# A hybrid encoder layer on one core: a written-out instruction order in place of a planner's, and four attention chunks held open

## The chip, the cores and the metric

The kernel runs on one core of a Trainium2 chip. The core has TensorE for matrix products (PE; its weight loads are listed as PEld), VectorE (DVE), ScalarE (ACT), GpSimd (POOL) and SyncE (SP), which issues most DMAs. Engines run their own instruction lists in order and wait for each other through semaphores. The metric is the device time of one execution in microseconds; before the change the median of three runs is 1474.67 us (1472.99 to 1477.0).

## The reference

One layer, 2048 tokens of width 1024, batch 1, all in f32:

```python
hn = rmsnorm(h, mix_norm_g)
u, g_ssm, q, k, v, g_attn = split(hn @ w_in)            # six parts of 512 columns
y_ssm = s5_branch(u, ...) * silu(g_ssm)                 # diagonal complex state space, 32 groups of 16 channels, then GELU and GLU
y_att = stick_breaking_branch(q, k, v, ...) * silu(g_attn)
h = h + concat([y_ssm, y_att]) @ w_out
h = h + sigmoid(rmsnorm(h) @ w_ple_gate) * (p @ w_ple_proj)
```

The attention has 8 heads of 64 and no softmax. For each query the weight of an earlier key is `sigmoid(z)` times the product of `sigmoid(-z)` over the keys between the two, strictly causal, in blocks of 128 queries. The S5 branch is a linear recurrence over time with complex state, computed in chunks.

## The kernel before, in words

Precision comes from splitting: an f32 matrix becomes a high and a low half in f32r, and `mm3` or `mm3x` adds three products of halves (lines 541 to 543 and 707 to 709). Where no split is made, plain f32 products run: the S5 products `ps_b` (L401) and `ps_y` (L461 to L464), the transposes `ps_pack` (L340, L352) and `ps_t` (L1000), and `ps_o` of the attention (L843).

The program is written stage by stage, in this order:

- `phase_u`: the tokens are loaded, normalised, transposed (`ps_x`) and split into `xt`; the 512 columns of `u` are computed (`ps_u`), 256 tokens at a time, and POOL stores them (`u<-uq`, L638). For the first 256 tokens the input comes already transposed (`load_plain`); their norms are found by `norms` through PE (`ps_row`, L579 and L585) and applied later. Beside it DVE computes the S5 constants in `ssm_chain`, some 250 short instructions.
- Eight S5 batches, each beside one `gate_unit`, which computes the S5 gates (`ps_sg`).
- The attention, 40 steps over four pairs of heads, the pairs 8 steps apart. `attn_proj` computes q, k, v and the gate of 128 tokens (`ps_q`, transposes `ps_tq`), each product cut in two halves of 64 rows that run side by side. `attn_block` handles 128 queries of a pair of heads. For each chunk of 512 keys, from the latest back, PE makes scores `ps_z`; ACT takes the sigmoid into `px` (L816); DVE forms the running products in place (L821); PE transposes `px` into `ps_wt` (L526, 64 x 64 pieces); ACT copies that to a `ws` tile (L835). The products with v, `ps_o` (L843), add up over all chunks in one PSUM bank. The code puts them out for `HOLD` chunks at a time, 128 rows by 64 columns each, which is the other way of halving the array.
- In the last ten attention steps the GLU of the S5 branch (`ps_g2`, `ps_v2`; the page shows these as `ps_g` and `ps_v`) and sums of weight blocks are worked in.
- `phase_out`: `mixed_pair` multiplies by `w_out` (`ps_h`), `gated_pair` transposes (`ps_t`) and multiplies by `w_ple_gate` (`ps_g`) and `w_ple_proj` (`ps_p`), seven products in place of eight, as in Strassen's scheme. `yr` are the split operands.

The order in which an engine runs its instructions is not that of the program. `arrange` takes the whole list, `plan` finds each instruction's dependences and gives it a length by a table in `duration`, `best_order` runs a list scheduler forwards and backwards six times and keeps the best of its own estimates, and `arrange` then fixes the order of every engine by a chain of dependences. Groups marked by `abreast` stay together. The rings that bound how far work runs ahead are sizes in one line: `PXB` (8 `px` tiles), `WSB` (5 `ws` tiles of 4 KB a partition).

[...]

Of the kernel before, what the change touches and what calls it, by code (L numbers as in the profile page):

```python
# [18 lines left out]
P = 128  # L19
# [4 lines left out]
G = 32  # L24
GH = 16
ST = 64
L = 16
# [13 lines left out]
XB, XTB, GTB, QSB, PXB, WSB, SWB, ROTB, STA, STB, STC, ALT, ALT0, ALT1, SSM_STEPS, SSM_DEPTH, PREP0, PXX, WSX, XTX, XT0 = 4, 2, 5, 5, 8, 5, 2, 2, 3, 2, 3, "o", 0, 30, 10, 2, 0, 0, 0, 0, 13  # L41
# [8 lines left out]
HOLD = 2  # L50
# [1231 lines left out]
def footprint(ap, offset, shape):  # L1282

    row = 1
    for n in shape[1:]:
        row *= n
    p0, m = offset // row, 1
    f = offset % row + sum((n - 1) * s for s, n in ap[1:] if s < 0)
    for s, n in ap[1:]:
        if s and n > 1:  # L1290
            m = sum(m << (abs(s) * k) for k in range(n)) if n * abs(s) > 64 or m != 1 or s not in (1, -1) else (1 << n) - 1
    return p0, p0 + ap[0][1], m << f


def duration(i, name, outs, ins, psum):

    n = max([a[1] for a in outs + ins] or [1])
    eng = str(i.engine).split(".")[-1]
    if name == "InstDMACopy":
        names = [a.bass_ap.tensor.name for a in i.ins if getattr(a, "bass_ap", None) is not None]  # L1300
        return (0.6 if eng == "Pool" else 0.45), (4.0 if any("ssm_w_glu" in k for k in names) else 0.0)
    if name == "InstMatmult":
        cols, kind = outs[0][1], ins[0][2]
        if i.is_transpose:
            return (0.031 if ins[0][0] <= 64 else 0.109), 0.11
        if "float32r" in kind or "bfloat16" in kind:
            return max(cols / 2400.0 + 0.0136, 0.107) / (2 if ins[0][0] <= 64 else 1), 0.11
        half = min(outs[0][0], ins[0][0]) <= 64
        return (0.5 if outs[0][0] <= 32 else 1 if half else 2) * max(cols / 1160.0, 0.056), 0.12
    if eng == "Activation":  # L1310
        return (0.05 if psum else 0.094) + n * 0.00083, 0.065 if psum else 0.03
    if eng == "Pool":
        if name == "InstTensorTensor" and "pow" in str(i.op).lower():
            return 0.35 + 0.15 * n, 0.08
        base, slope = {"InstMemset": (0.04, 0.0008), "InstTensorCopy": (0.4, 0.001), "InstTensorScalarPtr": (0.25, 0.001), "InstTensorScalarAffineSelect": (0.14, 0.0008)}.get(name, (0.12, 0.00186))
        return base + slope * n, 0.09
    if name == "InstTensorScalarPtr" and i.is_tensor_tensor_scan:
        return 0.05 + n * 0.0022, 0.03
    if name in ("InstMemset", "InstTensorCopy", "InstTensorScalarPtr") and not psum and not i_tt(i):
        return 0.07 + n * 0.0006, 0.03  # L1320
    return 0.07 + n * 0.00104, 0.03


def i_tt(i):

    return getattr(i, "is_scalar_tensor_tensor", False)


def plan(tc, pools):

    mybir_i = list(tc.nc.cur_bb.bb.instructions)
    first, last = 16512, 229344
    open_l, open_r, open_b, base, slots, spans, over, home, used = [], [], [], {}, {}, [], {}, {}, {}
    for p in sorted(pools, key=lambda p: p.id):
        kb = int(p.kb_per_partition_size() * 1024)
        sp = str(p.space).split(".")[-1]
        if sp == "DRAM":
            base[p.id] = 0
        else:
            side = open_b if sp == "PSUM" else open_r if "right" in str(p.side) else open_l  # L1340
            born = int(p.alloc_inst.name.split("-")[1])
            while side and side[-1][2] is not None and side[-1][2] < born:
                side.pop()
            at = side[-1][0] if side else 0 if side is open_b else last if side is open_r else first
            lo = at - kb if side is open_r else at
            end = p.release_inst
            side.append((lo if side is open_r else lo + kb, p.id, None if end is None else int(end.name.split("-")[1])))
            base[p.id] = lo
            for q, l2, h2, e2, s2 in spans:
                if sp == s2 and l2 < lo + kb and lo < h2 and e2 is not None and int(e2.name.split("-")[1]) < int(p.alloc_inst.name.split("-")[1]):  # L1350
                    over.setdefault(p.alloc_inst.name, []).append(e2.name)
            spans.append((p.id, lo, lo + kb, end, sp))
        for sp, size, tag, addr, _ in p.gen_slots(0):
            home[tag] = p.alloc_inst.name, p.release_inst.name if p.release_inst is not None else None
            slots.setdefault(tag, []).append((str(sp).split(".")[-1], base[p.id] + addr, size // P))
    turn, tiles, held, pre, length, opened, soft, mode = {}, {}, {}, [], [], {}, [], {}
    number = {i.name: k for k, i in enumerate(mybir_i)}
    for k, i in enumerate(mybir_i):
        if type(i).__name__ == "BassTilePoolBoundary":
            pre.append(set())  # L1360
            soft.append({number[q] for q in over.get(i.name, [])} | used.get(i.name, set()))
            length.append((0.0, 0.0, 0, False))
            continue
        need, ins, outs, loose, psum, read = set(), [], [], set(), False, 0
        for w, accs in ((0, i.ins), (1, i.outs)):
            for a in accs:
                b = getattr(a, "bass_ap", None)
                if b is None:
                    continue
                t, n = b.tensor, 1  # L1370
                ap = [(int(s), int(c)) for s, c in b.ap]
                for s, c in a.ap[1:]:
                    n *= int(c)
                (outs if w else ins).append((int(a.ap[0][1]), n, str(a.dtype)))
                read += not w and n > 1 and type(t).__name__ == "Tile" and slots_space(slots, t.tag) == "SB"
                if type(t).__name__ != "Tile":
                    continue
                shape = tuple(int(x) for x in t.shape)
                if t.name not in tiles:
                    mine = slots[t.tag]  # L1380
                    q = turn[t.tag] = turn.get(t.tag, -1) + 1
                    sp, lo, size = mine[-q % len(mine)]
                    tiles[t.name] = rec = (sp, [], [], k)
                    if t.tag in opened:
                        loose.add(opened[t.tag])
                    opened[t.tag] = k
                    if sp != "DRAM":
                        kept = []
                        for l2, h2, r2 in held.get(sp, []):
                            if l2 < lo + size and lo < h2:  # L1390
                                need.update(r2[2])
                                if lo <= l2 and h2 <= lo + size:
                                    continue
                            kept.append((l2, h2, r2))
                        held[sp] = kept + [(lo, lo + size, rec)]
                sp, accesses, users, born = tiles[t.name]
                loose.add(born)
                a0, r0 = home[t.tag]
                loose.add(number[a0])
                used.setdefault(r0, set()).add(k)  # L1400
                if sp == "PSUM":
                    psum = True
                    f = (0, P, 1)
                    w = 1
                elif sp == "DRAM":
                    row = shape[-1] if len(shape) < 3 else shape[1] * shape[2]
                    o = int(b.offset)
                    reach = o + sum((c - 1) * s for s, c in ap if s > 0)
                    f = (o // row, reach // row + 1, -1)
                else:  # L1410
                    f = seen_footprint(tuple(ap), int(b.offset), shape)
                kept = []
                for r in accesses:
                    j, wj, g = r
                    if j != k and (w or wj) and f[0] < g[1] and g[0] < f[1] and f[2] & g[2]:
                        need.add(j)
                        if w and f[0] <= g[0] and g[1] <= f[1] and (f[2] == -1 or (g[2] != -1 and not g[2] & ~f[2])) and sp != "DRAM":
                            continue
                    kept.append(r)
# [203 lines left out]
```

## Time and profile before

| what | value |
| --- | --- |
| median of three runs | 1474.67 us (1472.99 to 1477.0) |
| the profiled execution | 1474.24 us, its span 1472.5 us |
| mean granted TensorE clock | 0.994 |
| PE, DVE, ACT, POOL busy | 98%, 69%, 55%, 32% |
| instructions in the profile | 33586 |
| DMA traffic | 238.21 MB, 162 GB/s on the mean |

The stages by the profile: `phase_u` to about 125 us, S5 and gates to about 313, attention to about 1100, the GLU within its last 200, then `ps_h` to about 1250 and the gated product to the end. In rows of the profile "x16" counts instructions; a time is in us from the start of the span; PE shows two records for a plain f32 product that is not a transpose.

### The profile page before, as it was taken

Reading aid. Unit: us, or ns where it says so; the run is one execution under the profiler, and the core shown is the slowest. Engines: PE = TensorE matmul, PEld = TensorE weight load, DVE = VectorE, ACT = ScalarE, POOL = GpSimd, SP = SyncE. Lnnn points to the kernel's source line nnn. Section 1 sums busy time; section 2 is a strip of 40 time slices with the busy share of each in tenths; the row PEclk is TensorE's granted clock in tenths of the full one; section 3 lists DMA queues with packets and bytes.
Section 4 is the critical chain, followed back from the end, with each engine's and each line's share of the span. In section 5 each row is a group of like instructions: output and inputs, shape, how many; then the busy total and the mean of one; then the engine's idle time right before and its main releaser. Section 6 shows DMA issues by size and latency. Waiting matters only on the chain.

```text
span 1472.5 us, 33586 instructions
## 1 busy us (share of the span) xinstructions
PE 1436.7 (98%) x13068; PEld 1224.2 (83%) x13068; DVE 1009.0 (69%) x1817; ACT 810.4 (55%) x1765; POOL 474.8 (32%) x512
## 2 busy tenths in 40 slices
PE   6999999999999999999999999999999999999998
PEld 5999889988888888888888877777778888778786
DVE  8953977977567786678766775666778557754444
ACT  5654555565555766567655665555665345533432
POOL 3131363522221211221121124443334554534432
PEclk8999999999999999999999999999999999999999
DMA  8886845645333433334332455766568556523221
GB/s 289 288 287 205 250 143 186 206 143 168 128 130 125 144 112 114 114 130 140 121 126 102 142 146 171 226 218 178 155 201 280 176 171 200 166 65 101 93 72 58
DMA packets 179054, 238.21 MB, mean 162 GB/s; under 512 B 65760, under 2 KB 121296, under 8 KB 167760
## 3 DMA queue, kind: packets, MB, share of 16 engines
q1 hardware_dynamic: 176512, 227.49, 48.0%
q0 software_dynamic: 2384, 8.59, 2.0%
q8 instruction: 103, 1.69, 0.5%
q14 instruction: 55, 0.45, 0.1%
HBM read 166.94 MB, written 64.90 MB: 157 GB/s over the span
## 4 chain that ended last, share of the span: by engine, by line
PE 81%; DVE 7%; DMA 3%; ACT 3%; issue 3%; POOL 2%; SPq 1%; POOLq 0%; DVEq 0%; ACTq 0%
PE ps_q L745 21%; PE ps_o L843 7%; PE ps_z L812 6%; PE ps_wt L526 4%; PE ps_g L707 4%; PE ps_h L709 4%; PE ps_h L707 3%; PE ps_h L708 3%; PE ps_g L709 3%; PE ps_g L708 3%; DMA v<-qn 2%; PE ps_u L541 1%; PE ps_u L543 1%; PE ps_u L542 1%; PE ps_sg L541 1%
## 5 line engine op out<-in xcount | busy, mean ns | idle before, releaser
L821 DVE TENSOR_TENSOR_SCAN px<-px,ps_z 128x512 f32<-128x512 f32 (+3 forms) x320 | 339.9, 1086 | 85.9 <-ACT px L816 61.0
L745 PE MATMUL ps_q<-w_w,xt 64*128 64x512 f32 x2784 | 376.7, 399 | 1.3 <-DVE qn L65 0.7
L745 PEld LDWEIGHTS ps_q<-w_w,xt 64*128 64x128 f32 x2784 | 270.8, 185 | 39.7 <-DVE qn L65 2.2
L816 ACT ACTIVATE px<-ps_z 128x512 f32<-128x512 f32 (+3 forms) x320 | 159.2, 535 | 81.0 <-PE ps_z L812 79.8
L835 ACT ACTIVATE ws<-ps_wt 128x512 f32<-128x512 f32 (+3 forms) x320 | 160.7, 539 | 72.0 <-PE ps_wt L526 67.1
L812 PE MATMUL ps_z<-k,q 64*128 64x512 f32 (+3 forms) x960 | 137.7, 379 | 3.7 <-DVE px L821 1.8
L843 PE MATMUL ps_o<-ws,v 128*64 128x128 f32 x2176 | 134.9, 276 | 0.0
L843 PEld LDWEIGHTS ps_o<-ws,v 128*64 128x64 f32 x2176 | 117.3, 137 | 17.6 <-issue 14.7
L507 POOL TENSOR_TENSOR rs_qk<-rs_qk,mhalf 128x4 f32<-128x4 f32 x64 | 67.7, 1058 | 150.7 <-DVE rs_qk L72 148.1
L526 PEld LDWEIGHTS ps_wt<-ident,px 64*128 64x128 f32 x2176 | 95.5, 138 | 24.3 <-ACT ws L835 5.2
L812 PEld LDWEIGHTS ps_z<-k,q 64*128 64x128 f32 x960 | 87.9, 186 | 21.7 <-issue 5.4
L526 PE MATMUL ps_wt<-ident,px 64*128 64x64 f32 x2176 | 100.7, 224 | 2.0 <-ACT ws L835 1.8
L819 POOL TENSOR_SCALAR_AFFINE_SELECT px<-px 128x128 f32<-128x128 f32 x128 | 40.7, 328 | 164.2 <-ACT px L816 154.3
L756 POOL TENSOR_TENSOR v<-qn,v 128x128 f32<-128x128 f32 x64 | 32.2, 503 | 167.6 <-DMA v<-qn 153.9
L541 PE MATMUL ps_u<-xt,w_w 128*128 128x256 f32 x256 | 76.0, 298 | 7.5 <-ACT w_w L491 6.2
L65 DVE TENSOR_TENSOR yr<-sx,yr 128x512 fp32r<-128x512 f32 x64 | 50.6, 814 | 42.2 <-ACT yr L513 41.8
L543 PE MATMUL ps_u<-xt,w_w 128*128 128x256 f32 x256 | 74.5, 297 | 1.9 <-DVE w_w L76 1.8
L542 PE MATMUL ps_u<-xt,w_w 128*128 128x256 f32 x256 | 75.3, 295 | 0.5 <-DVE xt L65 0.5
L1032 POOL TENSOR_TENSOR sg<-sg,h 128x512 f32<-128x512 f32 x28 | 40.1, 1437 | 92.1 <-DVE sg L65 91.9
L513 ACT ACTIVATE yr<-sx 128x512 fp32r<-128x512 f32 x64 | 39.1, 627 | 53.7 <-POOL sx L912 22.6
L65 DVE TENSOR_TENSOR qn<-ps_q,part 128x512 f32<-128x512 f32 x54 | 36.8, 682 | 42.6 <-ACT part L751 39.0
L513 ACT ACTIVATE yr<-yq 128x512 fp32r<-128x512 f32 x48 | 30.2, 629 | 53.3 <-PE ps_h L709 24.5
(438 smaller groups left out, 3486.5 us busy)
## 6 DMA issues: line engine op xcount, KB each, us to landing
xt<-hn SPq DMA_DIRECT2D x58, 1024.0 KB
hn<-xt SPq DMA_DIRECT2D x16, 1024.0 KB
h<-h SPq DMA_DIRECT2D x64, 256.0 KB
wst<-in_w_in_dram SPq DMA_DIRECT2D x48, 256.0 KB
xg<-hn SPq DMA_DIRECT2D x12, 1024.0 KB
out_dram<-sg SPq DMA_DIRECT2D x31, 256.0 KB
x<-in_x_dram SPq DMA_DIRECT2D x14, 512.0 KB
h<-in_x_dram SPq DMA_DIRECT2D x28, 256.0 KB
```

Of the source, the lines that this page charges most:

```text
L526: e.nc.tensor.transpose(ps[h][:, 64 * k:64 * k + 64], v[r], e.ident[r, r])
L541: mm(out, wh, xh, start=first, stop=False)
L542: mm(out, wh, xl, start=False, stop=False)
L543: mm(out, wl, xh, start=False, stop=last)
L707: mm(out, xh, wh, start=first, stop=False, skip_group_check=more)
L709: mm(out, xl, wh, start=False, stop=last, skip_group_check=more)
L745: nc.tensor.matmul(o, xt[r, a, c], A.w[c][r, b], start=c + s == 0, stop=c == NC8 - 1 and s == 2)
L812: nc.tensor.matmul(z[:, :n], q[half[h], a], A.k[ch][half[h], b, :n], start=s == 0, stop=s == 2)
L816: nc.scalar.activation(px[:, :n], z[:, :n], AF.Sigmoid, scale=-(HD ** -0.5))
L821: nc.vector.tensor_tensor_scan(rv, rv, z[:, :n][:, ::-1], initial=1.0 if carry[h] is None else carry[h], op0=ALU.mult, op1=ALU.bypass)
L835: nc.scalar.activation(dst, ps, AF.Copy, bias=1.0, scale=-1.0)
L843: nc.tensor.matmul(po[half[h], :P], A.v[sb][:, h], w[:, h, b], start=sb == i, stop=sb == 0)
```

## The change

Every change is of order or size; each instruction computes what it did.

- The planner (`footprint`, `duration`, `plan`, `list_schedule`, `best_order` and helpers) is removed. `_ORDER` holds, packed as text, for each of the engines PE, DVE, ACT, POOL and SP a list of positions: which of the instructions that are left, in program order, comes next. `arrange` chains the engine's instructions in that order.
- `HOLD` goes from 2 to 4: the `ps_o` products of a block are written into the program after its last chunk, where before blocks with three or four chunks wrote them in two parts.
- `WSB` goes from 5 to 8: three more `ws` tiles.
- The scratch for POOL's descriptors goes from the default to 4096 bytes a partition, which frees the 12 KB of the three tiles.

```diff
-XB, XTB, GTB, QSB, PXB, WSB, SWB, ROTB, STA, STB, STC, ALT, ALT0, ALT1, SSM_STEPS, SSM_DEPTH, PREP0, PXX, WSX, XTX, XT0 = 4, 2, 5, 5, 8, 5, 2, 2, 3, 2, 3, "o", 0, 30, 10, 2, 0, 0, 0, 0, 13
+XB, XTB, GTB, QSB, PXB, WSB, SWB, ROTB, STA, STB, STC, ALT, ALT0, ALT1, SSM_STEPS, SSM_DEPTH, PREP0, PXX, WSX, XTX, XT0 = 4, 2, 5, 5, 8, 8, 2, 2, 3, 2, 3, "o", 0, 30, 10, 2, 0, 0, 0, 0, 13
-HOLD = 2
+HOLD = 4
-def footprint(ap, offset, shape):
...
-    return best
+_ENGINES = ("PE", "DVE", "Activation", "Pool", "SP")
+_ORDER = (
...
+)
+def written_order(ops):
+    import base64, zlib
+    code = iter(zlib.decompress(base64.b85decode(_ORDER)))
+    for e in _ENGINES:
+        left = [i for i in ops if type(i).__name__ != "BassTilePoolBoundary" and str(i.engine).split(".")[-1] == e]
+        line = []
+        while left:
+            at, shift, c = 0, 0, 128
+            while c & 128:
+                c = next(code)
+                at |= (c & 127) << shift
+                shift += 7
+            line.append(left.pop(at))
+        yield line
 def arrange(tc, pools, rows):
-    ops, pre, *rest = plan(tc, pools)
-    _, order, _ = best_order(ops, pre, *rest, rows)
     info = mybir.DependencyInfo(mybir.DependencyClass.NoSync, mybir.DependencyReason.DATA)
-    for line in order.values():
+    for line in written_order(list(tc.nc.cur_bb.bb.instructions)):
         for a, b in zip(line, line[1:]):
-            tc.add_manual_dep(ops[b], ops[a].name, info, reason="arrange")
+            tc.add_manual_dep(b, a.name, info, reason="arrange")
-    nc = _bacc.Bacc("TRN2", target_bir_lowering=False, num_devices=1)
+    nc = _bacc.Bacc("TRN2", target_bir_lowering=False, num_devices=1, dynamic_dma_scratch_size=4096)
```

More of the change, by code (lines that the diff above doesn't have):

```diff
@@ L1279, in hybrid_block_kernel @@
     wstack.close()
-def footprint(ap, offset, shape):
[L1284 to L1321, printed above, removed]
```

280 lines of the change are left out of this document (70 added, 210 removed).

## The prediction

> **What bounds the kernel now.** First the head of the page, with the totals and the chain of work that ended last:
>
> ```profile
> span 1472.5 us, 33586 instructions
> PE 1436.7 (98%) x13068; PEld 1224.2 (83%) x13068; DVE 1009.0 (69%) x1817; ACT 810.4 (55%) x1765; POOL 474.8 (32%) x512
> ...
> PE 81%; DVE 7%; DMA 3%; ACT 3%; issue 3%; POOL 2%; SPq 1%; POOLq 0%; DVEq 0%; ACTq 0%
> ```
>
> TensorE is the bound: busy 98% and 81% of the chain; no other engine is over 69%. A busy PE isn't one at its peak, so the second view cuts the span by stage; the number behind each x is what to compare.
>
> ```profile
> core 0: us, PE busy (x) PEld busy (x) DVE busy (x) ACT busy (x) POOL busy (x), PEclk, DMA share, GB/s
> 0.00:20.00 20.00, 11.87 (x66) 11.01 (x67) 15.99 (x101) 9.25 (x17) 5.45 (x16) 0.98 0.79 266
> 20.00:40.00 20.00, 14.57 (x99) 13.00 (x98) 19.19 (x88) 14.05 (x24) 9.76 (x12) 0.68 0.84 315
> 40.00:60.00 20.00, 20.00 (x206) 19.20 (x205) 19.36 (x103) 13.84 (x24) 1.87 (x3) 1.00 0.82 268
> ...
> 100.00:310.00 210.00, 207.44 (x1694) 196.54 (x1693) 154.05 (x268) 111.96 (x253) 79.56 (x48) 1.00 0.61 190
> 310.00:1080.00 770.00, 759.27 (x8731) 635.23 (x8730) 533.30 (x876) 463.71 (x1082) 195.30 (x297) 1.00 0.46 145
> ```
>
> PE's idle time is in the first 40 us (165 products where 20 us of the next stretch hold 206, and a clock of 0.68 in the second row). From 100 us on it never rests for long. So a new order can win little by closing holes; it must make the same 13068 products stream denser. The next view, PE's instructions in order of time, shows where they don't. What to read is the distance from the start of a row to the start of the next.
>
> ```profile
> 136.00 0.38 PE L352 MATMUL ps_pack<-ident,lt 128*128 128x128 f32 x2
> 136.13 0.36 PE L541 MATMUL ps_sg<-xt,w_w 128*128 128x256 f32 x1
> ...
> 139.80 1.95 PE L401 MATMUL ps_b<-us,stB 128*128 128x128 f32 x16
> 141.50 0.36 PE L541 MATMUL ps_sg<-xt,w_w 128*128 128x256 f32 x1
> ...
> 1386.89 0.60 PE L1000 MATMUL ps_t<-ident,h 128*128 128x128 f32 x4
> 1387.24 0.48 PE L707 MATMUL ps_g<-w_w,yr 128*128 128x512 f32 x1
> ...
> 1393.73 0.60 PE L1000 MATMUL ps_t<-ident,h 128*128 128x128 f32 x4
> 1394.66 0.50 PE L707 MATMUL ps_g<-w_w,yr 128*128 128x512 f32 x1 [0.34 <-ACT yr L513]
> ```
>
> Plain f32 products on the whole array cost 0.13 us for a run of 2, 0.35 for 4, 1.70 for 16: (1.70 - 0.13) / 14 = 0.112 us for each further one, while the run as a whole is 2 x 0.112 - 0.13 = 0.09 us cheaper than that price. One product of each run is almost free, since the f32r product behind it starts 0.02 to 0.03 us later. So the same f32 products, cut into more runs with f32r products between, take less PE time. (The last pair shows the other kind of loss: 0.93 us where 0.35 would do, with a wait for `yr`.)
>
> The attention stage, same view, then PE's weight-load waits, then two pieces of the chain:
>
> ```profile
> 441.47 0.96 PE L745 MATMUL ps_q<-w_w,xt 64*128 64x512 f32 x6
> 442.36 2.62 PE L843 MATMUL ps_o<-ws,v 128*64 128x128 f32 x44
> ...
> 445.91 2.91 PE L745 MATMUL ps_q<-w_w,xt 64*128 64x512 f32 x24
> 448.67 0.30 PE L526 MATMUL ps_tq<-ident,qn 64*128 64x64 f32 x4
> ...
> 450.31 0.85 PE L812 MATMUL ps_z<-k,q 64*128 64x512 f32 x6
> 450.99 0.66 PE L526 MATMUL ps_wt<-ident,px 64*128 64x64 f32 x16
> 451.46 0.71 PE L745 MATMUL ps_q<-w_w,xt 64*128 64x512 f32 x4
> ```
>
> ```profile
> PEld ps_o L843 <- issue: 14.7, 42, 0.4
> PEld ps_g L707 <- ACT yr L513: 7.5, 17, 1.6
> ...
> PEld ps_wt L526 <- issue: 5.1, 21, 0.4
> PEld ps_z L812 <- DVE px L821: 4.3, 12, 1.7
> ```
>
> ```profile
> 727.61 3.64 PE ps_o L843 x64
> ...
> 1081.99 1.90 PE ps_o L843 x32
> ```
>
> `ps_o` uses the array by halves of columns, all else there by halves of rows. Inside a run one `ps_o` product costs (3.64 - 1.90) / 32 = 0.054 us, so a run pays 1.90 - 32 x 0.054 = 0.16 us for leaving; before it six `ps_q` took 0.89 us where 24 took 2.76, that is 0.20 us over. A run of `ps_o` thus costs about 0.36 us beside its products. The weight loads stand still 14.7 / 42 = 0.35 us on entering and 5.1 / 21 = 0.24 on leaving, 0.59 together, the upper bound.
>
> **The change part by part.** No instruction is added or removed on any engine; the diff changes their order, `HOLD`, one ring (`WSB`: five to eight `ws` tiles, not raw-weight stages) and the scratch. The list in the diff was decoded against the program order of before, with the `ps_o` products of a block put together at its end as `HOLD = 4` does, and laid beside the planner's order. Counts below are from these two lists.
>
> 1. Runs of plain f32 products standing between f32r products (`ps_y`, `ps_b`, `ps_pack` between `ps_sg`; `ps_t` between `ps_g`, `ps_p`): 83 in the planner's order, 201 in the written one, with 109 runs of a single product against 9. 118 x 0.09 = 10.6 us on PE, in stages where PE is the path. Bounds 0 (if the cover fails for single products) and -10.6. I take four fifths, -8.5, since the runs shown behind a wait give their gain back.
>
> 2. Runs of `ps_o`: 73 become 65, because blocks with three or four chunks no longer put theirs out in two parts. 8 x 0.36 = 2.9 us, at most 8 x 0.59 = 4.7. I take -3. The eight `ws` tiles are what lets four chunks wait; they cost 12 KB a partition and no time.
>
> 3. Waits of PE in the attention. Between the end of a `ps_z` product and the first `ps_wt` that needs its result stand ACT and two scans on DVE:
>
> ```profile
> L821 DVE TENSOR_TENSOR_SCAN px<-px,ps_z 128x512 f32<-128x512 f32 (+3 forms) x320 | 339.9, 1086 | 85.9 <-ACT px L816 61.0
> ...
> L816 ACT ACTIVATE px<-ps_z 128x512 f32<-128x512 f32 (+3 forms) x320 | 159.2, 535 | 81.0 <-PE ps_z L812 79.8
> L835 ACT ACTIVATE ws<-ps_wt 128x512 f32<-128x512 f32 (+3 forms) x320 | 160.7, 539 | 72.0 <-PE ps_wt L526 67.1
> ```
>
> 0.54 + 2 x 1.09 = 2.7 us if nothing queues. Summing PE's products between the two at the distances above (0.115 for `ps_q`, 0.11 `ps_z`, 0.03 `ps_wt`, 0.054 `ps_o`), the median cover is 6.9 us in the planner's order and 11.2 in the written one; the lowest quarter ends at 5.1 and 7.6. The wait `ps_z` for `px` (4.3 us, the bank isn't scanned yet) is the one next in line: a bank is asked for again after a median of 3.7 us in the old list and 3.5 in the new, so it stays. I take -3; bounds -7 (the waits of loads on `px` and `ws` all gone) and +10 (each of the 64 blocks 0.16 us more, the cost of one exit).
>
> 4. Last stage: runs of `ps_p` products, which need nothing of the pair before, go from 31 to 106, spread between `ps_g` and `ps_t` and partly brought forward. They cover part of the 7.5 us that loads waited for `yr`. -2, bounds 0 and -7.5.
>
> 5. The start:
>
> ```profile
> 24.14 0.38 PE L579 MATMUL ps_row<-ones,x 128*128 128x1 f32 x2 [0.69 <-POOL x L577]
> ...
> 34.81 0.58 PE L542 MATMUL ps_u<-xt,w_w 128*128 128x256 f32 x1 [0.51 <-DVE xt L65]
> ```
>
> ```profile
> 37.10 0.21 PE ps_u L542
> ...
> 39.66 0.12 PE ps_u L542
> ```
>
> PE's first product of the norms stands 21st in the written order and 85th in the planner's, the transposes of the next pair 72nd instead of 100th, and DVE makes the eighth low half of the weights as its 130th instruction instead of 110th; SP sends six x pieces ahead of the first weight instead of two. If the norms come at 24.14 as now, 75 products of 0.12 us stand behind them: 24.1 + 9.0 + the transposes = 34, against 34.8 for the next pair's start; the transposes come sooner, the weights later. I take 0, bounds -3 (the norms' squares start earlier) and +6 (the same 75 at 0.21 us, the step under the low clock, take 6.8 us more: 40.8).
>
> 6. The scratch for software-made descriptors, a quarter of before. Only POOL's DMAs use it, 22 in all; the largest are the `u` stores:
>
> ```profile
> u<-uq POOLq DMA_DIRECT2D x8, 512.0 KB, 7.8
> ```
>
> No view shows the fill of a ring. If each store waited for the one before it to land, POOL would lose up to 7.8 us a store; a row scale of the next tile stands behind the first four, POOL then waited 4.36 us for DVE anyway:
>
> ```profile
> 83.82 2.60 POOL L507 TENSOR_TENSOR rs_x<-rs_x,mhalf 128x1 f32<-128x1 f32 x1 [4.36 <-DVE rs_x L72]
> ```
>
> Bounds 0 and 2 x 7.8 - 4.4 = +11. I take 0, nearest to what the row of 83.82 shows: POOL is ahead of DVE there. [...]
>
> Sum: -8.5 - 3 - 3 - 2 + 0 + 0 = -16.5. The profiled execution took 1474.24 us (span 1472.5), which is 0.43 under the median 1474.67. 1474.24 - 16.5 = 1457.7; I forecast 1458.
>
> **The rivals.**
> - B, cutting the f32 runs brings nothing. In the trace single f32 products hardly occur, so the row stops at runs of two, and where both neighbours also load weights the load may have no cover. Then term 1 is 0 and the time 1466. For it: the single run of one in the last stage comes with a wait; against it: the price is the same 0.09 for runs of 2, 4 and 16, in two stages. [...]
> - C, nothing measurable. PE's 98% would be true work, or a full ring in term 6 (+11) with a slow start (+6) eats the 16.5: about 1475. Against it: the distances above.
> - D, slower. With all `ps_o` at the end of a block, PE arrives there with its last transposition just done and must wait for ACT to copy `ws`, then the next block's bank for `y`. The price is 64 blocks times the wait; it decides from (16.5 + 4.4) / 64 = 0.33 us a block, and at 0.4 the time is 1458 + 25.6 = 1484. For it: the cover between a chunk's transposes and its `ps_o` is no longer than before (lowest 5% at 3.4 us in both lists). Against it: ACT's two copies of a chunk need 2 x 0.54 = 1.1 us of that.
> - E, waits go too: terms 1 to 4 at their ends, 10.6 + 4.7 + 7 + 7.5 = 29.8; the waits of terms 3 and 4 stand partly at the runs of terms 1 and 2, so I count 27 of it: 1447.
>
> **How the numbers follow.** Forecast (1450 to 1463) 0.48, B 0.20, C 0.10, D 0.10, E 0.12. 0.3% of this time, 4.4 us, is about what a measurement here can tell from none. Forecast, B and E lie below 1470.2: faster 0.80; C: same 0.10; D: slower 0.10. The range goes from 1446, under E, to 1472, over B and to the near edge of C; it leaves out D and most of C.
>
> **What would show it.** Term 1: rows of `ps_y`, `ps_b`, `ps_pack`, `ps_t` with x1 or x2 and an f32r row 0.02 to 0.03 us after the last; more products per us than 1694 in 210 in the stage from 100 to 310. Term 2: `ps_o` rows of up to x64 from one block, and fewer issue waits than 42 of its loads. Term 3: the wait of `ps_wt` and `ps_o` loads on `px` and `ws` no longer than now. Term 4: the wait on `yr` under 7.5. Term 5: the first product of the second pair near 34 us. Term 6: no gap after the `u` stores on POOL. The prediction is wrong if the f32 rows stand as singles 0.11 us apart, if POOL stalls at the stores, or if `ps_o` loads wait on `ws` in most blocks.

## The result and the profile after

The kernel after took 1514.25 us (median of 4 runs, 1513.25 to 1515.84) against 1474.95 us (4 runs, 1472.99 to 1477.0): ratio 1.0267, 95% interval 1.0249 to 1.0285. It is 39.3 us slower; 1458 was forecast, with 1472 as the upper end. The head of its page, totals and the chain of work that ended last:

```profile
span 1511.5 us, 33486 instructions
...
PE 1434.3 (95%) x13068; PEld 1223.3 (81%) x13068; DVE 1031.1 (68%) x1817; ACT 807.4 (53%) x1765; POOL 466.4 (31%) x512
...
PE 71%; DVE 12%; issue 6%; DMA 5%; ACT 4%; POOL 2%; SPq 0%; POOLq 0%; DVEq 0%; ACTq 0%
```

PE's work is the same (13068 products, 1434 us of busy time against 1437), but its share of the chain fell from 81% to 71%; DVE went from 7% to 12%, issue from 3% to 6%. PE waits where it did not. The second view, cut by stretches of time (busy time and count of PE, PEld, DVE, ACT and POOL, then the granted clock, the DMA share and GB/s), says where:

```profile
20.00:40.00 20.00, 13.96 (x117) 13.22 (x117) 19.55 (x70) 14.57 (x24) 9.04 (x11) 0.77 0.51 182
40.00:60.00 20.00, 17.20 (x153) 16.07 (x153) 18.97 (x81) 9.56 (x17) 1.65 (x3) 0.91 0.64 242
60.00:80.00 20.00, 13.76 (x112) 13.06 (x112) 19.21 (x73) 9.22 (x17) 1.80 (x3) 0.84 0.57 208
80.00:100.00 20.00, 20.00 (x172) 19.53 (x171) 15.32 (x22) 9.12 (x17) 3.71 (x3) 0.91 0.89 298
100.00:120.00 20.00, 7.47 (x81) 6.87 (x79) 2.33 (x5) 2.68 (x4) 6.03 (x5) 0.78 0.71 211
120.00:140.00 20.00, 17.92 (x145) 17.42 (x146) 5.74 (x11) 11.55 (x24) 1.64 (x3) 0.80 0.49 185
```

The kernel before made 206 products from 40 to 60 us. For the two last stretches its rows are:

```profile
100.00:120.00 20.00, 20.00 (x187) 19.60 (x186) 4.30 (x8) 9.12 (x18) 1.10 (x2) 1.00 0.51 201
120.00:140.00 20.00, 20.00 (x172) 19.45 (x171) 7.70 (x11) 7.16 (x16) 4.68 (x4) 1.00 0.83 244
```

81 products stand where 187 stood. Following the ends of stages in the two traces, the 768th and last `ps_u` product comes at 169.0 us instead of 128.9 (40 late), the last `ps_o` at 1137.2 instead of 1098.9 (38 late), the end of the span at 1511.5 instead of 1472.5 (39 late). The whole lag is there by the end of the `u` products, and stays (some 50 gate products were made before that end, so the gate stage loses their time again). The largest hole, engines in order of time:

```profile
93.58 1.24 POOL L638 DMA_DIRECT2D u<-uq  x1 [2.73 <-ACT uq L635]
...
100.24 0.15 DVE L72 TENSOR_SCALAR rs_x<-ss 128x1 f32<-128x1 f32 x1
...
100.86 1.17 POOL L638 DMA_DIRECT2D u<-uq  x1 [6.04 <-issue]
...
107.19 0.28 PE L543 MATMUL ps_u<-xt,w_w 128*128 128x256 f32 x1
107.56 1.15 POOL L638 DMA_DIRECT2D u<-uq  x1 [5.53 <-issue]
114.65 1.16 POOL L638 DMA_DIRECT2D u<-uq  x1 [5.94 <-issue]
115.82 2.03 POOL L333 TENSOR_TENSOR tm<-pwi,cts 128x1024 f32<-128x1024 f32 x1
117.81 0.56 POOL L507 TENSOR_TENSOR rs_x<-rs_x,mhalf 128x1 f32<-128x1 f32 x1
118.40 1.15 ACT L598 ACTIVATE x<-x,rs_x 128x1024 f32<-128x1024 f32 x1 [14.78 <-POOL rs_x L507]
...
121.10 1.29 DVE L65 TENSOR_TENSOR xt<-ps_x,xt 128x512 fp32r<-128x512 f32 x2 [0.26 <-ACT xt L513]
...
121.85 0.37 PE L526 MATMUL ps_x<-ident,x 64*128 64x64 f32 x1 [14.38 <-DVE xt L65]
```

POOL issues a `u` store at 93.58 and then stands 6.04, 5.53 and 5.94 us ahead of the next three, on nothing that the profile shows ("issue"). A row scale whose input DVE had ready at 100.24 + 0.15 is run by POOL at 117.81, behind the stores and one product. ACT's scaling of x, DVE's `xt` and PE's next transposition (after 14.38 us) follow in a row.

### The profile page after: what moved, and what is told of

Its sections match the earlier page's. It is cut to its first block, busy times and chain, and to the rows that moved or that the text cites. A ratio compares the mean times of both kernels' runs of the same rounds, so it can differ in the third digit from the quotient of the medians.

```text
span 1511.5 us, 33486 instructions
## 1 busy us (share of the span) xinstructions
PE 1434.3 (95%) x13068; PEld 1223.3 (81%) x13068; DVE 1031.1 (68%) x1817; ACT 807.4 (53%) x1765; POOL 466.4 (31%) x512
## 3 DMA queue, kind: packets, MB, share of 16 engines
q0 software_dynamic: 2384, 8.59, 2.1%
## 4 chain that ended last, share of the span: by engine, by line
PE 71%; DVE 12%; issue 6%; DMA 5%; ACT 4%; POOL 2%; SPq 0%; POOLq 0%; DVEq 0%; ACTq 0%
PE ps_q L745 18%; PE ps_o L843 7%; PE ps_z L812 5%; PE ps_wt L526 4%; PE ps_g L707 3%; PE ps_g L709 3%; PE ps_g L708 3%; PE ps_h L709 3%; PE ps_h L707 3%; PE ps_h L708 3%; DMA wst<-in_ssm_w_glu_dram 2%; DVE px L821 1%; PE ps_u L542 1%; PE ps_u L541 1%; PE ps_u L543 1%
## 5 line engine op out<-in xcount | busy, mean ns | idle before, releaser
L745 PE MATMUL ps_q<-w_w,xt 64*128 64x512 f32 x2784 | 370.2, 398 | 0.9 <-DVE qn L76 0.7
L835 ACT ACTIVATE ws<-ps_wt 128x512 f32<-128x512 f32 (+3 forms) x320 | 155.3, 538 | 86.2 <-PE ps_wt L526 83.2
L526 PEld LDWEIGHTS ps_wt<-ident,px 64*128 64x128 f32 x2176 | 90.0, 139 | 34.4 <-ACT ws L835 13.6
L541 PE MATMUL ps_u<-xt,w_w 128*128 128x256 f32 x256 | 71.0, 306 | 14.8 <-ACT w_w L491 11.0
L542 PE MATMUL ps_u<-xt,w_w 128*128 128x256 f32 x256 | 71.8, 303 | 4.9 <-DVE xt L65 4.9
L543 PE MATMUL ps_u<-xt,w_w 128*128 128x256 f32 x256 | 69.1, 301 | 2.4 <-DVE w_w L76 2.4
L65 DVE TENSOR_TENSOR yr<-sx,yr 128x512 fp32r<-128x512 f32 x64 | 58.6, 934 | 17.9 <-ACT yr L513 17.2
L541 PEld LDWEIGHTS ps_u<-xt,w_w 128*128 128x128 f32 x256 | 51.0, 211 | 15.6 <-ACT w_w L491 11.0
```

The source lines that it names most:

```text
L65: nc.vector.tensor_tensor(out, a, b, op=op)
L526: e.nc.tensor.transpose(ps[h][:, 64 * k:64 * k + 64], v[r], e.ident[r, r])
L541: mm(out, wh, xh, start=first, stop=False)
L745: nc.tensor.matmul(o, xt[r, a, c], A.w[c][r, b], start=c + s == 0, stop=c == NC8 - 1 and s == 2)
L835: nc.scalar.activation(dst, ps, AF.Copy, bias=1.0, scale=-1.0)
```

## The experiments

"Planner's order" is the order of before; where two orders are joined, each engine's list is put together from the two lists, and nothing else is changed. Such edits are shown as lines on the lists. Times in brackets are ratios to the kernel before run on the same chip, with 95% intervals. In short: the ring (the scratch for POOL's descriptors) costs 9 us, the written order of the start 26, that of the gate stage 7 to 9, and everything behind 310 us nothing.

**The small scratch alone.**

```diff
-    nc = _bacc.Bacc("TRN2", target_bir_lowering=False, num_devices=1)
+    nc = _bacc.Bacc("TRN2", target_bir_lowering=False, num_devices=1, dynamic_dma_scratch_size=4096)
```

> The kernel before (planner's order, HOLD 2, five ws tiles) with the scratch of software-made descriptors cut to 4096 and nothing else. Theory A (the small ring makes POOL stand still at the u stores): in the kernel after, three of the first four u stores stood 6.0, 5.5 and 5.9 us with nothing to wait for. Here a row scale stands between the first store and the second and the fourth store is issued at 79, the next row scale at 83.8, so about 18 us of standing less the slack around them leaves 5 to 15 us: 1480 to 1490, and rows on POOL of 5 to 6 us of issue ahead of the stores. Rival (the standing in the kernel after came from something else, such as the stores being back to back with other traffic): no issue time ahead of the stores and 1475 +-2.

1486.01 us (1.0060, 1.0045 to 1.0076): 9 us lost, as theory A says. POOL's rows:

```profile
85.75 1.15 POOL L638 DMA_DIRECT2D u<-uq  x1 [6.90 <-ACT xt L513]
96.42 1.16 POOL L638 DMA_DIRECT2D u<-uq  x1 [9.52 <-issue]
97.60 0.56 POOL L507 TENSOR_TENSOR rs_x<-rs_x,mhalf 128x1 f32<-128x1 f32 x1
```

One store waits 9.52 us for issue with the row scale behind it at 97.60; in the kernel before the row scale ran at 83.82. PE's 576th `ps_u` product comes 10 us late and the 10 us stay to the end. What a store waits for can be read off the landings, though the profile names no releaser: the first three stores land at 77.17, 85.44 and 96.11 us, and the next ones are issued at 77.65, 85.75 and 96.42. Here and in the kernel after, a store that follows another is issued 0.3 to 0.5 us after that one has landed, in all twelve cases; in the kernel before, the third store goes out at 77.07, 8 us before the second lands at 85.06.

**The scratch, `HOLD` and the eight `ws` tiles, still planned.**

```diff
-XB, XTB, GTB, QSB, PXB, WSB, ... = 4, 2, 5, 5, 8, 5, ...
+XB, XTB, GTB, QSB, PXB, WSB, ... = 4, 2, 5, 5, 8, 8, ...
-HOLD = 2
+HOLD = 4
```

> The same with HOLD 4 and eight ws tiles besides, still under the planner. To be read against the run with the small scratch alone. Theory: blocks open between attention steps and the eight tiles are worth little, -3 to +3 us against that run. Rival (PE waits at the ends of blocks): 64 blocks at 0.1 to 0.3 us, +6 to +20 us, in the stage from 300 to 1090 us.

1538.48 us (1.0413, 1.0394 to 1.0433), 52 us above the run with the small scratch alone: both theories missed, the rival by a factor of two and more. 44 of it lie between the first `ps_q` and the last `ps_o` product, 830 us here:

```profile
322.00:1152.00 830.00, 790.35 (x8934) 659.48 (x8935) 536.17 (x882) 470.98 (x1095) 197.11 (x306) 0.97 0.43 136
```

The clock is 0.97 there, and the longest waits of PE are `ps_wt` for `ws` (8.4 us) and the GLU's gate products for `zr` (7.1 us, three waits). So four open blocks and eight tiles are no help in themselves: the planner's own order for them is far worse, and the written one brings that back to even (below).

**The `u` stores on SP, in the kernel after.**

```diff
-                nc.gpsimd.dma_start(e.u_d[ct][:, :, c0:c0 + NCH // 2].rearrange("j p c -> p j c"), uq[ct])
+                nc.sync.dma_start(e.u_d[ct][:, :, c0:c0 + NCH // 2].rearrange("j p c -> p j c"), uq[ct])
```

> The kernel after with its eight u stores issued by SP's queue instead of POOL's, same written order otherwise. Theory A: the 14.7 us in which PE stood after 107 us go, and the second set's standing (5 us at three stores) too: -17 to -23 us, 1491 to 1497; the rest, +16 to +22 against before, is the start (13 to 17 us) and the stage of the mixed pairs (10), less 9 in the last stage. Rival (the wait comes from the order, which puts the row scale behind all four stores): the scale still comes late because SP stands instead, 1508 to 1514.

1505.44 us (1.0189, 1.0174 to 1.0204): 8.8 us come back by the medians, 11.5 by the ratios, about half of what was expected. The hole of 14.7 us shrinks to 5.2 and not to nothing: ACT then stood 10.64 us for a weight still to be loaded (`wst`), whose load stands behind the `u` stores in SP's list. The ring is worth about 9 us in both kernels, and 28 to 30 us are left.

**The last stage alone, in the written order, on the kernel before** (full scratch, `HOLD` 2).

```diff
 every engine, planner's order
-instructions of the output projection and per-layer gate: planner's order
+instructions of the output projection and per-layer gate: written order, in the same places of the list
```

> The order of before with the full scratch, HOLD 2 and five ws tiles, but the instructions of the last stage (output projection and per-layer gate) in the written order of after among themselves. Theory C (cutting the runs of plain f32 transposes in the last stage is worth what it costs a run, and the last stage of after took 214 us against 223): -6 to -9 us, 1466 to 1469, provided that the stage of the mixed pairs does not lose its 10 us here. If those 10 us come from the written order of that stage itself: 1474 to 1478, with the loss visible before the last ps_h product. Rival: the cut is worth nothing and both stages stay: 1475 +-2.

1478.46 us (1.0007, 0.9997 to 1.0016): nothing. The 9 us by which the last stage of after is shorter are `ps_p` products done earlier (the first at 1128.4 us here, at 1250.4 in the kernel before), among the mixed pairs, which last that much longer: the last `ps_h` product comes 14 us later.

**Where the remaining 30 us are, from both ends.** Every list starts with what the planner put into its first 126 us (up to the last `ps_u`), then follows the written order:

```diff
 u stores on SP, HOLD = 4, WSB = 8, scratch 4096
-every engine: written order
+every engine: planner's first 126 us, then the rest in the written order
```

> The kernel after with SP issuing the u stores, and every engine's list cut in two: first all that the planner had put into its first 126 us (to the last ps_u product), in the planner's order, then the rest in the written order. HOLD 4, eight ws tiles, scratch 4096. Theory (all of the loss is the order of the start and the ring; from the first ps_sg product on the written order takes as long as the planner's): 1505.4 less 30 = 1475, 1471 to 1479. Rival 1 (the rest of the written order gains its 16 us once the start is right): 1458 to 1465. Rival 2 (the rest loses too): above 1483.

1483.39 us (1.0064, 1.0043 to 1.0085): 18 of the 28 us are gone by the ratios, 22 of the 30 by the medians; rival 2, by a little. The same cut behind the last `ps_sg`, so that only attention, mixed pairs and last stage are as written, with `HOLD` 4 and eight tiles:

```diff
-every engine: planner's first 126 us, then the rest in the written order
+every engine: planner's first 306 us, then the rest in the written order
```

> The kernel after with u stores on SP and the planner's order for everything up to the last ps_sg product (its first 306 us); the written order only from there: attention with HOLD 4 and eight ws tiles, mixed pairs and last stage; scratch 4096. Theory (the cut at 126 us kept 7.5 us of loss, which is the written order of the gate stage, and attention and last stage are worth nothing): 1474 to 1478. Rival 1 (attention or last stage give part of the predicted gain of 8 us): 1466 to 1471. Rival 2 (the 7.5 us are lost in the attention or in the last stage): 1481 to 1485.

1476.66 us (1.0001, 0.9990 to 1.0012, 12 runs): what the written order, the four open blocks and the eight tiles do after 310 us is worth 0.1 us, between -1.5 and +1.8. The difference of the two, 7 to 9 us, is the written order of the gate stage. PE's longest waits in that stage in the run with the cut at 126 us:

```profile
PE ps_pack L352 <- ACT lt L349: 3.0, 1, 3.0
PE ps_qk L707 <- DVE gsq L65: 2.0, 1, 2.0
PE ps_sg L541 <- DVE sg L65: 1.9, 3, 1.5
```

In the kernel before the longest one of that stage is 0.6 us. And the mirror, the order of before with only the start as written (full scratch, `u` stores on POOL):

```diff
 every engine, planner's order
-instructions of phase_u, its chain and the gate weights' loads: planner's order
+instructions of phase_u, its chain and the gate weights' loads: written order, in the same places of the list
```

> The mirror: the order of before with the full scratch, HOLD 2, five ws tiles and u stores on POOL, but the instructions of the start (loads, norms, turned x, u products, weights of the gate stage) in the written order among themselves. Theory (the written order of the start costs about 30 us by itself): 1500 to 1508. Rival (the start is late only because of the ring or the later stages): 1475 to 1485.

1501.4 us (1.0179, 1.0164 to 1.0194): the written start alone costs 26 us. With the ring (9), the gate stage (7 to 9) and nothing behind it, that makes 42 to 45 where 39 were measured; part of the ring's standing may fall into time that the start loses anyway, which no run separates.

**Which decision of the start?** The first 40 us in the planner's order, the written one from there (on the kernel after, `u` stores on SP):

```diff
-every engine: planner's first 126 us, then the rest in the written order
+every engine: planner's first 40 us, then the rest in the written order
```

> The same cut at the planner's 40 us: the planner's order for the first 40 us, the written one from there. In the kernel after, the 96th ps_u product ends at 38.7 us against 25.8 (13 us late), the 768th at 159.2 against 128.9 with the u stores on SP (30 late). If the two losses are separate: 1505.4 - 13 = 1492. If the later one follows from the first 40 us (the low clock after the idle time, or DVE late with the x halves): 1475 to 1480. If the first 13 us are won back anyway: 1503 to 1506.

1500.94 us (1.0172, 1.0157 to 1.0188): -4.5, so most of the first 13 us is won back by itself: the 288th `ps_u` product, 39.4 us behind the 96th in the run with the `u` stores on SP, is 46.3 us behind it here (72.2 against 25.9 us). SP's own order alone:

```diff
-SP: x, x, x, x, x, x, wst, gmix, wst, wst, x ...
+SP: gmix, x, x, wst, wst, x, x, wst, wst ...
```

> The kernel after with u stores on SP, and only SP's own DMAs of the start in the planner's order (gmix first, two x pieces and then the first weight, instead of six x pieces ahead of it); DVE, ACT, POOL and PE as written. If the late first weight is what costs (ACT's first w_w at 10.2 us instead of 5.4): -4 to -6, about 1500. If the order of DVE, POOL and PE costs (norms ahead of the transposes): within 2 us of 1505.4.

1513.95 us (1.0263, 1.0246 to 1.0280): 8.5 us worse, neither theory. ACT's list still wants six x pieces before the first weight, SP now sends them later, and PE's first product waits 16.5 us instead of 11.2. Twelve DVE instructions moved back:

```diff
 DVE, as written
-  ... cts, pr_den, pwis, pr_fr, bb, bbs, pr_fis, tb ... rs_x, xt (third pair) ... xt (fourth pair)
+  ... rs_x, xt (third pair) ... xt (fourth pair), pr_den, cts, pr_fis, pr_fr, bb, tb, bbs, pwis
```

> The kernel after with u stores on SP, and on DVE alone twelve instructions of the state-space preparation (cts, pwis, pr_den, pr_fr, pr_fis, bb, bbs, tb) put back behind the halves of the fourth pair's x, where the planner has them; in the written order they run at 31 to 49 us, before the third pair's. By the rows of the kernel after they take 0.48 + 0.35 + 0.50 + 0.18 + 0.43 + 6 x 0.69 = 6.1 us of DVE. Theory (DVE's order is what makes PE wait 3.3, 3.6 and 5.2 us for x halves at 71, 75 and 104 us): -5 to -9 against 1505.4, that is 1496 to 1500. Rival (PE waits for something else there, or the tables come too late for the gate stage instead): 1503 to 1508.

1511.26 us (1.0231, 1.0214 to 1.0249): 6 us worse. The waits only changed places: PE stands 3.1 and 3.3 us at 69 and 72 us, and 2.5 us at 92 and again at 107. Four further runs on the mirror (full scratch, 1501.4 us) take one candidate each. Two copies on ACT ahead of a scaling that stands for POOL (the rows are those of the kernel after):

```profile
71.70 1.15 ACT L598 ACTIVATE x<-x,rs_x 128x1024 f32<-128x1024 f32 x1 [5.31 <-POOL rs_x L507]
72.76 1.07 ACT L513 ACTIVATE xt<-ps_x 128x512 fp32r<-128x512 f32 x2
```

```diff
-ACT: x (scaled, 5th pair), jk, x (scaled, 5th pair, second half), xt, xt (4th pair, second half)
+ACT: x (scaled, 5th pair), xt, xt (4th pair, second half), jk, x (scaled, 5th pair, second half)
```

> The kernel of the mirror (order of before, the start as written; 1501.4 us) with one change on ACT: the two copies of turned x of the fourth pair's second half stand ahead of the square and the scaling of the fifth pair's second half, as the planner has them, instead of behind. In the kernel after, ACT stood 5.31 us there for POOL's row scale while both copies could have gone, and PE then waited 3.3 and 3.6 us. Theory: -4 to -7, 1494 to 1497. Rival (PE then waits for the next late x instead): 1499 to 1503.

1505.1 us (1.0190, 1.0175 to 1.0205): no gain. SP's and ACT's first 26 us:

```diff
-SP, ACT: the start as written
+SP, ACT: the start's first 26 us in the planner's order, then as written
```

> The mirror (1501.4 us) with SP's and ACT's lists in the planner's order for the first 26 us, DVE, POOL and PE as written: x pieces and weights alternate again, on the queue and on ACT. Theory (the first product at 11.0 us instead of 6.2 is the loss): -4 to -6, 1495 to 1498. Rival (DVE's late low halves of the weights and PE's early norms hold the start anyway): 1499 to 1503.

1511.01 us (1.0231, 1.0216 to 1.0246): 8 to 10 us worse: PE starts at 6.5 us, but the norms, for which it stands at the same place of its list, come at 31.0 us instead of 23.3. All queues but PE's:

```diff
-SP, ACT, DVE, POOL: the start as written
+SP, ACT, DVE, POOL: the start's first 26 us in the planner's order, then as written
```

> The mirror with SP, ACT, DVE and POOL in the planner's order for the first 26 us and only PE as written, so that PE still meets the norms' products 21st of its list. If the early norms on PE are the loss (7.3 us of standing at 16 us): 1496 to 1501 still. If the loads and the low halves are: the 96th ps_u product near 28 us instead of 39.7 and -8 to -12, 1489 to 1493.

1500.75 us (1.0163, 1.0148 to 1.0178). PE in order of time:

```profile
11.06 0.41 PE L542 MATMUL ps_u<-xt,w_w 128*128 128x256 f32 x1
25.05 0.37 PE L579 MATMUL ps_row<-ones,x 128*128 128x1 f32 x1 [13.57 <-POOL x L577]
```

With everything else in the planner's order PE reaches the norms at 11 us and stands 14 us for them; the 96th `ps_u` product comes at 38.7 us, as in the kernel after. The early place of the norms in PE's list is the whole lag at 40 us. Yet with PE's first 40 us put right too, and the two copies:

```diff
-every engine: the start as written
+every engine: planner's first 40 us, then the start as written; ACT: xt, xt ahead of jk and x as above
```

> The mirror with the planner's order on all engines for the first 40 us, and besides the two copies on ACT ahead of the scaling. Theory (the two are the whole loss of the start): within 4 us of before, 1475 to 1480. If the first 40 us are won back later (as -4.5 in the run of the kernel after with the old 40 us suggests), or a third late x follows: 1485 to 1497.

1500.1 us (1.0162, 1.0142 to 1.0182): next to no gain over all, although the 96th product is back at 26.1 us. The fourth pair's x is late again, and the trace says on which queue:

```profile
67.14 1.08 ACT L513 ACTIVATE xt<-ps_x 128x512 fp32r<-128x512 f32 x2 [7.21 <-PE ps_x L526]
...
75.30 1.28 DVE L65 TENSOR_TENSOR xt<-ps_x,xt 128x512 fp32r<-128x512 f32 x2
...
76.63 0.58 PE L542 MATMUL ps_u<-xt,w_w 128*128 128x256 f32 x1 [4.46 <-DVE xt L65]
```

ACT's two copies of that x are done at 68.2; DVE adds its part at 75.30, 7 us later, behind state-space instructions. The same x is held up in two in-order queues, so that moving it on one of them gains nothing. On both at once:

```diff
 planner's first 40 us, ACT: xt, xt ahead of jk and x
-ACT: jk, x (5th pair, second half), uq, uq, uq     DVE: state-space instructions, xt, xt (4th pair, second half)
+ACT: uq, uq, uq, jk, x (5th pair, second half)     DVE: xt, xt (4th pair, second half), state-space instructions
```

> The run with the planner's first 40 us and the copies first (1500.1 us), and besides: on ACT three evictions of u ahead of the fifth pair's square, on DVE the two additions that finish the fourth pair's x at the planner's place in the list (291st) and the twelve state-space instructions behind them. Theory (the same x is held up in two in-order queues, so that either repair alone gains nothing): the 288th ps_u product at 64 to 70 us instead of 76.6, and -6 to -12, 1488 to 1494. Rival (the time is lost again at 105 to 112 us whatever comes before): 1498 to 1502.

1495.8 us (1.0122, 1.0105 to 1.0139): 4 to 6 us gained, the 288th product at 70.8 instead of 76.6 us; a little less than expected, as PE still stands 6.3 us at 64.5. The planner's order up to 80 us:

```diff
-every engine: the start as written
+every engine: planner's first 80 us, then the start as written
```

> The order of before with the start as written only from the planner's 80 us on; everything earlier in the planner's order. What is left is the place at 105 to 112 us, where PE waits 3.0 and 2.7 us for x and the clock then falls to 0.61 for 10 us. Theory (the places add up once each is the only one): 5.7 us of waits and some 4 us of slow clock, 1481 to 1487. Rival (all of the loss sits in the third place): 1496 to 1502; or none: 1475 to 1479.

1482.38 us (1.0035, 1.0024 to 1.0046), as the theory has it. From the ratios, with the places put right in this order: 2 to 3 us of the written start's 26 belong to the first 40 us (the rest of their lag is won back), 18 to the stretch from 40 to 80, 5 to what follows. The 5 us can be read off PE's rows of this last run:

```profile
90.82 0.39 PE L541 MATMUL ps_u<-xt,w_w 128*128 128x256 f32 x1
94.90 0.58 PE L541 MATMUL ps_u<-xt,w_w 128*128 128x256 f32 x1 [3.70 <-ACT uq L635]
95.28 0.41 PE L542 MATMUL ps_u<-xt,w_w 128*128 128x256 f32 x1
95.49 0.41 PE L543 MATMUL ps_u<-xt,w_w 128*128 128x256 f32 x1
...
99.33 0.41 PE L541 MATMUL ps_u<-xt,w_w 128*128 128x256 f32 x1
...
100.02 0.28 PE L542 MATMUL ps_u<-xt,w_w 128*128 128x256 f32 x1
100.14 0.29 PE L543 MATMUL ps_u<-xt,w_w 128*128 128x256 f32 x1
```

```profile
90.00:100.00 10.00, 6.30 (x44) 5.90 (x43) 2.08 (x3) 2.67 (x5) 2.53 (x2) 0.66 0.91 338
100.00:110.00 10.00, 10.00 (x95) 9.80 (x94) 2.86 (x5) 6.50 (x12) 0.55 (x1) 1.00 0.37 119
```

PE stands 4.1 us between two starts (it waits 3.70 us for an eviction by ACT), and for 4.9 us after it the products stand 0.21 us apart instead of 0.12, at a clock of 0.66 over these 10 us: 23 products times 0.09 us, 2 us more. This hole is paid one and a half times.

**Mending the ring.** The scratch at 8192:

```diff
-    nc = _bacc.Bacc("TRN2", target_bir_lowering=False, num_devices=1)
+    nc = _bacc.Bacc("TRN2", target_bir_lowering=False, num_devices=1, dynamic_dma_scratch_size=8192)
```

> The kernel before with the scratch at 8192. If the standing at the u stores falls with the number of stores that the ring holds: one store in flight at 4096, two at 8192, so the second store of each four goes at once and the third stands; less than half of the 20.4 us of issue time ahead of the stores, and 1476 to 1480. If 8192 holds all four: no issue time and 1475.

1479.94 us in a single run, within what the kernel before showed on that chip (1474.11 to 1480.05); no issue time ahead of any `u` store, and up to three stores in flight at once (the fourth goes out at 80.80, the second and third land at 85.59 and 88.19). So it is 4096 that is too short, for stores of 512 KB. And 4096 with the `u` stores on SP, in the planner's order:

```diff
 planner's order, scratch 4096
-                nc.gpsimd.dma_start(e.u_d[ct]...)
+                nc.sync.dma_start(e.u_d[ct]...)
```

> The order of before, HOLD 2 and five ws tiles, with the scratch at 4096 and the u stores issued by SP. Theory (the u stores are all that the small ring hurts, and SP has room for them): 1474 to 1478, and no loss at 104 to 114 us. Rival (the four yq and four h loads that POOL issues before the last stage stand too, or SP's own loads come late behind the stores): 1479 to 1486.

1477.04 us (1.0005, 0.9996 to 1.0014): no loss, so the `u` stores are all that the small ring hurt. No version here is faster than the kernel before; this one equals it with the scratch at 4096.

## Why the prediction was wrong

Rival C had the mechanisms, "a full ring in term 6 (+11) with a slow start (+6)", at half their price (17 us against 35) and with a chance of 0.10. Rival D alone had the direction, also at 0.10, but not the cause: in the kernel after, loads of `ps_o` wait 1.2 us in all for `yat` and for no `ws` tile, and everything behind 310 us is even with the kernel before.

- **Term 1 (-8.5), wrong in its price.** The step that failed is "the run as a whole is 2 x 0.112 - 0.13 = 0.09 us cheaper". The distance to the next f32r product was taken as the end of the bill. The row that follows the two of 136.00 and 136.13 in the kernel before, and a single f32 product in the kernel after, in order of time:

```profile
136.34 0.28 PE L542 MATMUL ps_sg<-xt,w_w 128*128 128x256 f32 x1
```

```profile
1332.10 0.39 PE L708 MATMUL ps_g<-w_w,yr 128*128 128x512 f32 x1
1332.33 0.27 PE L1000 MATMUL ps_t<-ident,h 128*128 128x128 f32 x1
1332.36 0.47 PE L708 MATMUL ps_g<-wx,yr 128*128 128x512 f32 x1
1332.67 0.39 PE L707 MATMUL ps_g<-w_w,yr 128*128 128x512 f32 x1
```

The f32r product behind the run starts 0.13 us after it, but the one behind that 0.21 us later instead of 0.12: 0.34 for two f32 products and one f32r, just 2 x 0.112 + 0.12. In the kernel after a single `ps_t` between two `ps_g` takes 0.57 from `ps_g` to the second next `ps_g`, 0.23 + 0.11 + 0.23. (That one product also lasts longer, 0.36 against 0.28 us and 0.47 against 0.39; the 0.36 stood in a row that the prediction quoted.) Counted in this way over the whole last stage of the kernel after, 36 single `ps_t` cost a median of 0.12 us each and ten runs of four 0.45. An f32 product costs its 0.11 to 0.12 us alone or in a run; cutting 83 runs into 201 is worth nothing, as rival B had it. The "same 0.09 for runs of 2, 4 and 16" that was held against it was read from half a pair, and the whole pair no longer says so. The reason rival B gave, a load that "may have no cover", is not shown either: no run here takes the load by itself, and from 100 to 310 us, where most products use the whole array, loads are listed as busy for 196.54 us beside 207.44 us of products in 210 us.

- **Terms 2 and 3 (-6): the sign of the waits was half right, the sum 0.** The loads of PE that waited, in the kernel after:

```profile
PEld ps_wt L526 <- ACT ws L835: 13.6, 42, 3.2
...
PEld ps_wt L526 <- issue: 9.5, 40, 0.4
PEld ps_o L843 <- issue: 8.0, 23, 0.4
PEld ps_z L812 <- DVE px L821: 7.7, 8, 2.2
...
PEld ps_g L707 <- ACT yr L513: 1.3, 4, 0.6
```

`ps_o` is entered 23 times with a wait instead of 42, 8.0 us instead of 14.7, as term 2 said; on leaving, `ps_wt` loads stand 9.5 us, 40 times, where it was 5.1 and 21. And the waits of `ps_wt` for `ws`, of which term 3 expected less, rose to 13.6 us; before, these and the waits for `px` were:

```profile
PEld ps_wt L526 <- ACT ws L835: 5.2, 9, 0.9
...
PEld ps_wt L526 <- ACT px L816: 0.5, 3, 0.2
```

`ps_z` for `px` went from 4.3 to 7.7. The step of term 3 that failed is the choice of the distance: the cover from `ps_z` to `ps_wt` guards a wait for `px` that cost 0.5 us to begin with. What grew is the wait until ACT has copied earlier transposes out of their PSUM banks into `ws`, which that sum does not hold. In the run whose attention is as written, 8949 products take 787 us, against 785 for the same 8949 in the kernel before.

- **Term 4 (-2): the wait on `yr` fell from 7.5 to 1.3 us** as predicted, and came back as waits of `ps_h` for `yr` (4.1 and 2.1 us) among the mixed pairs, to which part of the `ps_p` products had been brought forward. Sum 0, as the run with the last stage alone shows (1.0007).

- **Term 5 (0, bounds -3 and +6): +26.** The step that failed is the count of one place, the norms: "24.1 + 9.0 + the transposes = 34". The second pair's first product came at 39.8 us, inside that step's own bounds (to 40.8). (It comes at 33.72 in the kernel before; the row of 34.81 is the pair's second.) Two things were left out. The lists were costed only to that product, although DVE, which had 19.36 us of work in the 20 us that follow, had its instructions reordered for 40 us more; 18 of the 26 us are there. And only the upper bound, for 75 products, had the low clock in it, which came back with later holes (0.91 and 0.84 from 40 to 80 us, where it was 1.00).

- **Term 6 (0, bounds 0 and +11): +9.** The bound was right, the choice not. The step that failed is "nearest to what the row of 83.82 shows": the 4.36 us in which POOL waited for DVE covers one store, and three stand. The condition behind the bound, "If each store waited for the one before it to land", is what the runs show, at about 6 us a store. (POOL issues 25 DMAs in the trace, not 22, which changes nothing; their 8.59 MB are all that the queue listed as software_dynamic moves in the kernel before.)

Of the signs under "What would show it", the gap at the `u` stores is there, and so are single f32 products at 0.11 us each; `ps_o` loads that wait on `ws` are not.

## What to carry to other kernels

Price a pipelined instruction over its whole neighbourhood, from one steady step to the next: a cheap row can be paid for in the row behind (here 0.13 us, then 0.21 instead of 0.12). When an order is replaced, walk every queue through the stage with least slack to its end, and look for the same operand waiting in two in-order queues, since repairing one of them can show nothing. Where the cover of a cost is a wait elsewhere, count how often the cost comes before the cover is used up.

## What the runs showed of the hardware

- With the scratch for POOL's descriptors at 4096, each 512 KB store that followed another was issued only 0.3 to 0.5 us after that one had landed, and in nine of the twelve cases (six in the kernel after, three in the run with the small scratch alone) POOL stood 4.0 to 9.5 us for it on nothing that the profile shows; at 8192, in a single run, three were in flight at once and none stood.
- In the run with the planner's first 80 us, after PE stood 4.1 us between two starts, its products went at 0.21 instead of 0.12 us for 4.9 us (granted clock 0.66 from 90 to 100 us). A shorter hole was followed by a clock of 0.50 in one kernel and of 1.00 in another, so here the length of a hole alone does not tell what it costs. PE stood 1.81 us between two starts at 16.40 us in the kernel before and at 16.55 us in the run with the planner's first 80 us; the same stretch behind it, in this order:

```profile
19.10:22.40 3.30, 3.30 (x17) 3.30 (x16) 3.30 (x14) 2.92 (x4) 1.70 (x2) 0.50 0.68 278
```

```profile
19.10:22.40 3.30, 2.60 (x21) 2.36 (x20) 3.30 (x14) 2.78 (x4) 1.55 (x2) 1.00 0.64 263
```

- The planner's order with four open blocks and eight tiles is 52 us slower than with two and five. Why its waits grow so was not tried further. Nor was it settled which other places of the stretch from 40 to 80 us hold the 12 to 15 us that moving one x on two queues left.
